# A gate of plain products, with the block sums of the next product made while it runs

## The chip, the cores and the metric

The kernel runs on one core of a Trainium2 chip. A core has five engines that work side by side and wait for one another by semaphores: TensorE (PE) multiplies matrices and puts the sums into PSUM, VectorE (DVE) and ScalarE (ACT) work on tiles of 128 partitions, GpSimd (POOL) does a few elementwise operations, and SyncE (SP) issues the transfers from memory. Each engine runs its own instructions strictly in the order of the program.

The metric is the device time of one execution in microseconds (us). The kernel before took 1316.55 us, the median of three runs from 1316.47 to 1319.54.

## The reference

Two decoder layers over 512 tokens of width D = 1024. Layer 0 mixes by a linear recurrence and a sparse attention, layer 1 by latent attention; both are followed by the same three steps, which are what matters here:

```python
for i in range(2):
    m = mixer_i(x)
    h = layer_norm(ALPHA * x + m, ln1_g[i], ln1_b[i])
    f = square(relu(h @ mlp_w1[i])) @ mlp_w2[i]                   # 1024 -> 4096 -> 1024
    e = sigmoid(h @ ple_w_gate[i]) * (p[i] @ ple_w_proj[i])       # the gate, and the embedding
    x = layer_norm(ALPHA * h + f + e, ln2_g[i], ln2_b[i])
```

Everything is in fp32.

## The kernel before

Activations are held transposed: a tile has 128 features as partitions and 512 tokens as columns. The residual is eight tiles `y[0]` to `y[7]`, which stay in SBUF. Steps that are split by tokens take a left and a right half of 256 columns (`H`).

A product in fp32 is made of three faster ones: each operand is split into a high part (a copy rounded to the faster type) and a low part (the rest), and PE adds high x high, high x low and low x high. Splits of weights are made on the chip: ACT casts the high part, DVE subtracts for the low one (L89, L90, L751, L752). Weights arrive as 1 MB tiles `wraw`; the pool `wp` has two buffers each for the raw tile, its high part `whi` and its low part `wlo`.

Two helpers multiply by weights.

- `gemm_t` (L113) makes plain products: a weight tile is a group of 48 matmuls of 512 columns, three (L107, L108, L109) for each of 8 row blocks k and 2 output tiles. With `lead` its first two groups run side by side, k by k, so that a product can start on the first operands that are ready; with `halves` holding "lead" those two groups run first on the left 256 columns and then on the right. `wload` (L88) loads and splits a weight tile, and is given a slightly higher priority (`ahead=30`).
- `seven` (L730) cuts weights and activations into 2 x 2 blocks and makes seven block products in place of eight, each of 12 matmuls of 256 columns (L786): 84 matmuls a group. Its operands are sums and differences of blocks. For the weights DVE makes them in `front` (a third pair of buffers in the pool `third` belongs to it), for the activations `Norm.blocks` makes them once. ACT and DVE add the products together again afterwards (L797 and the lines behind it).

`Norm` (L201) is the layer norm. The first norm of a layer (`norm a`) works by halves of tokens: a sum over features by PE (L256), which is taken off each `y` on DVE; squares on ACT, added on DVE (L252); statistics by PE (L269, two matmuls a half), a root on ACT, and a spread over partitions by PE (L283). Then `blocks` (L329) applies it: for each row block DVE scales (L350), ACT and DVE make the high and low part with the bias (L344, L345), ACT keeps h itself in `n_h` (L355), and POOL writes ALPHA x h into `y` (L356). When the right half is done, four row blocks of block differences follow, four instructions each (L361 to L364) and their splits (L341, L342). The seven operands lie in the tiles `xb`.

After the norm a layer runs: `embed` (p times `ple_w_proj`, kept in eight tiles `pp`, L821), then `mlp` (L841): the gate by `seven` in four groups with `evg` (tanh on ACT, a product with `pp` and a sum into `y` on DVE), then four parts, each `mlp_w1` by `seven` in four groups (`ev1`: relu and square on ACT, a split) and `mlp_w2` by `gemm_t` (`ev2`: a sum into `y`). In the last part `ev2` feeds `norm b`, which uses one pass over the sums and makes the h of the next layer.

Tiles of the seven-product operands take the places `h` had: pool `res` has 16 of them, pool `mp` 12. The end loop (L1089) opens the pools of a layer: `norm a`'s around the output projection and the embedding, then `norm b`'s and `third` around `mlp`.

The order of the work is the program's order on each engine, set by a scheduler at build time: what comes first in the code comes first, unless it isn't ready, and weights' splits are drawn forward by their priority (`high_priority(120)` in `seven`, 30 in `wload`). PSUM has six banks in rotation for products and two for the norm.

## Time and profile before

| | |
|---|---|
| median of three runs | 1316.55 us |
| profiled execution | 1319.66 us |
| its span | 1317.8 us |
| TensorE (PE) matmuls busy | 1228.2 us, 93% |
| PE weight loads (PEld, beside the matmuls) | 1083.4 us, 82% |
| VectorE (DVE) busy | 989.8 us, 75% |
| ScalarE (ACT) busy | 702.3 us, 53% |
| GpSimd (POOL) busy | 205.1 us, 16% |
| instructions | 19322 |

The span runs from the first instruction to the last; the 1.9 us by which the execution is longer lie around it. A busy share is an average over stages, and matmuls overlap: the next begins before the end of the one before is shown, so what a matmul costs is read from the distance of two starts. The granted clock (PEclk) is 1.00 at 2.4 GHz and 0.50 at 1.2 GHz. Instructions are named by the line of the kernel that makes them, and many lines are helpers.

### The profile page before, as it was taken

What the parts mean: (1) busy time and instruction counts of PE and PEld (TensorE: products, weight loads), DVE (VectorE), ACT (ScalarE), POOL (GpSimd) and SP (SyncE); (2) the same over time, 40 slices, a digit from 0 to 9 for tenths busy, and PEclk for the clock granted to TensorE, in tenths of its full rate; (3) what the DMA queues carried; (4) which work ended last, traced back from release to release, by engine and by line L of the source; (5) the groups of instructions that cost most, each with busy time, mean ns of one, the idle gap of its engine ahead of it and who ended that gap; (6) DMA issues with size and microseconds to landing.
All of it is one profiled execution on the core that took longest, in us unless ns stands there. A gap on an engine that the chain in (4) does not pass through costs nothing.

```text
span 1317.8 us, 19322 instructions
## 1 busy us (share of the span) xinstructions
PE 1228.2 (93%) x7400; PEld 1083.4 (82%) x7400; DVE 989.8 (75%) x1925; ACT 702.3 (53%) x1306; POOL 205.1 (16%) x237
## 2 busy tenths in 40 slices
PE   7997889399999999999899999994999999999998
PEld 6685678299889899898796888793998898998987
DVE  5799978999658376585838898679996584764857
ACT  4465765644526245263356988637455263452633
POOL 1457550100000000000544442101000000000000
PEclk9798999699999999999889999997999999999999
DMA  6221120033323223233112010120333232232311
GB/s 209 96 70 59 65 81 33 0 103 123 115 78 129 96 85 108 96 120 104 34 68 96 33 33 17 65 79 18 101 116 117 84 129 96 83 110 67 126 65 64
DMA packets 20925, 111.01 MB, mean 84 GB/s; under 512 B 2464, under 2 KB 6560, under 8 KB 8640
## 3 DMA queue, kind: packets, MB, share of 16 engines
q1 hardware_dynamic: 20736, 109.18, 24.6%
q8 instruction: 58, 0.95, 0.3%
q0 software_dynamic: 96, 0.59, 0.2%
q14 instruction: 35, 0.29, 0.1%
HBM read 107.66 MB, written 2.10 MB: 83 GB/s over the span
## 4 chain that ended last, share of the span: by engine, by line
PE 74%; DVE 16%; ACT 7%; issue 2%; DMA 0%; POOL 0%; ACTq 0%; SPq 0%; DVEq 0%; POOLq 0%
PE ps L786 29%; PE ps L107 12%; PE ps L108 12%; PE ps L109 12%; ACT l L408 2%; DVE mb L568 1%; DVE m L567 1%; PE ps L421 1%; DVE xb L342 1%; PE ps L897 1%; ACT whi L89 1%; PE ps L898 1%; PE ps L896 1%; DVE n_s L252 1%; DVE wlo L752 1%
## 5 line engine op out<-in xcount | busy, mean ns | idle before, releaser
L786 PE MATMUL ps<-xb,whi 128*128 128x256 f32 x1512 | 279.1, 286 | 0.2 <-ACT whi L751 0.2
L786 PEld LDWEIGHTS ps<-xb,whi 128*128 128x128 f32 x1512 | 239.4, 194 | 1.6 <-ACT whi L751 0.4
L786 PE MATMUL ps<-xb,wlo 128*128 128x256 f32 x756 | 215.0, 286 | 1.2 <-DVE wlo L752 1.2
L107 PE MATMUL ps<-ah,whi 128*128 128x512 f32 (+1 forms) x544 | 206.7, 380 | 0.0
L108 PE MATMUL ps<-al,whi 128*128 128x512 f32 (+1 forms) x544 | 206.5, 380 | 0.0
L109 PE MATMUL ps<-ah,wlo 128*128 128x512 f32 (+1 forms) x544 | 205.4, 378 | 0.0
L89 ACT CAST whi<-wraw 128x1024 fp32r<-128x1024 f32 (+3 forms) x146 | 122.1, 873 | 138.0 <-PE ps L108 114.4
L90 POOL TENSOR_TENSOR wlo<-wraw,whi 128x512 fp32r<-128x512 f32 (+2 forms) x54 | 93.4, 1747 | 456.4 <-ACT whi L89 456.4
L786 PE MATMUL ps<-xb,wh 128*128 128x256 f32 x728 | 131.7, 282 | 34.3 <-ACT u L797 17.5
L786 PEld LDWEIGHTS ps<-xb,wlo 128*128 128x128 f32 x756 | 146.4, 194 | 2.2 <-DVE wlo L752 2.2
L786 PEld LDWEIGHTS ps<-xb,wh 128*128 128x128 f32 x728 | 111.9, 190 | 35.4 <-ACT u L797 17.7
L869 DVE TENSOR_TENSOR y<-y,ps 128x512 f32<-128x512 f32 (+1 forms) x68 | 44.3, 654 | 128.3 <-PE ps L109 128.1
L751 ACT CAST whi<-wraw 128x512 fp32r<-128x512 f32 (+1 forms) x54 | 45.0, 832 | 158.3 <-PE ps L108 92.1
L107 PE MATMUL ps<-hh,whi 128*128 128x512 f32 (+1 forms) x304 | 112.7, 373 | 8.9 <-ACT hh L89 5.8
L108 PEld LDWEIGHTS ps<-al,whi 128*128 128x128 f32 x544 | 103.0, 189 | 19.9 <-DVE al L90 1.2
L107 PEld LDWEIGHTS ps<-ah,whi 128*128 128x128 f32 x544 | 102.9, 189 | 19.8 <-ACT ah L89 1.2
L109 PEld LDWEIGHTS ps<-ah,wlo 128*128 128x128 f32 x544 | 102.9, 189 | 18.7 <-issue 0.5
L109 PE MATMUL ps<-hh,wlo 128*128 128x512 f32 (+1 forms) x304 | 111.4, 369 | 6.7 <-POOL wlo L90 6.0
L108 PE MATMUL ps<-hl,whi 128*128 128x512 f32 (+1 forms) x304 | 112.8, 371 | 1.8 <-POOL hl L90 1.8
L90 DVE TENSOR_TENSOR wlo<-wraw,whi 128x1024 fp32r<-128x1024 f32 (+1 forms) x92 | 96.6, 1081 | 15.7 <-ACT whi L89 15.6
L786 PE MATMUL ps<-xb,wl 128*128 128x256 f32 x364 | 102.0, 281 | 1.0 <-DVE wl L752 1.0
L107 PEld LDWEIGHTS ps<-hh,whi 128*128 128x128 f32 x304 | 59.4, 196 | 19.4 <-ACT hh L89 6.4
(328 smaller groups left out, 2546.4 us busy)
## 6 DMA issues: line engine op xcount, KB each, us to landing
wraw<-in_mlp_w SPq DMA_DIRECT2D x64, 1024.0 KB, 4.8
wraw<-in_w_out SPq DMA_DIRECT2D x8, 1024.0 KB, 4.8
wraw<-in_w_gate SPq DMA_DIRECT2D x8, 1024.0 KB, 4.9
wraw<-in_w_in SPq DMA_DIRECT2D x6, 1024.0 KB, 4.8
wraw<-in_w_ukv SPq DMA_DIRECT2D x4, 1024.0 KB, 4.7
wraw<-in_w_in SPq DMA_DIRECT2D x16, 128.0 KB, 3.8
y<-in_xT SPq DMA_DIRECT2D x8, 256.0 KB, 4.0
wraw<-in_w_proj SPq DMA_DIRECT2D x2, 1024.0 KB, 4.8
```

Of the source, the lines that this page charges most:

```text
L89: (act or nc.scalar.copy)(hi, src)
L90: (sub or nc.vector.tensor_sub)(lo, src, f(hi))
L107: nc.tensor.matmul(ps, whi, xhi, start=start, stop=False)
L108: nc.tensor.matmul(ps, whi, xlo, start=False, stop=False)
L109: nc.tensor.matmul(ps, wlo, xhi, start=False, stop=stop)
L252: nc.vector.tensor_add(self.s2[:, cs], self.s2[:, cs], sq[:, cs])
L342: nc.vector.tensor_sub(t[:, H:], src, f(t[:, :H]))
L408: nc.scalar.activation(L[blk], L[blk], AF.Exp, bias=mx[:, NB + blk:NB + blk + 1], scale=self.scale, accum_out=sums[:, blk:blk + 1])
L421: nc.tensor.transpose(ps[t][:, c:c + P], self.L[blk][:, kb * P:(kb + 1) * P], ident)
L751: nc.scalar.copy(hi, src)
L786: nc.tensor.matmul(o, u[:, c], v, start=start and k == n == 0, stop=k == 3 and n == 2, skip_group_check=True)
L869: nc.vector.tensor_add(y[n][:, cs], y[n][:, cs], ps[:, cs])
```

## The change

- **The gate by plain products.** `mlp` calls `gemm_t` for the gate, with `lead=8, halves=("lead",)`: the first two of its four groups run side by side, first on the left 256 columns, then on the right, and the other two on all 512. Its operands are the high and low parts of h, which `norm a` now makes for all eight row blocks, in `res`, like `norm b`. The evaluation `evg` takes tanh and multiplies with `pp` by halves for the first four outputs.
- **Block differences during the gate.** `blocks` and `new_x` go. The new `Norm.sums` makes the four differences and their splits, of `y` as it is (scaled, without bias; where the bias doesn't cancel it is joined in the same instruction, `db` being the difference of two biases). `evg` calls it at output 3, right half. The other three operands of the seven products are halves of h's own tiles, so `product` takes pairs (`xh`, `xl`).
- **ALPHA joined to later sums.** POOL's multiplication goes for `norm a`. `y` becomes `ALPHA * y + pp` in one instruction of `evg`, and ALPHA times the bias (`ab`, made in `first`) is added with the sum of part 0's `mlp_w2`.
- **Pools.** `third` is opened in `mlp` and closed ahead of the last `mlp_w2`, where `norm b`'s pool then takes its memory.

```diff
@@ Norm.first @@
             if self.onepass:
                 self.centre()
+            else:
+                b = small[:, self.base + 8:self.base + 16]
+                self.db, self.ab = (const.tile([P, n], F32, name=nm("b")) for n in (4, 8))
+                nc.vector.tensor_sub(self.db, b[:, 4:], b[:, :4])
+                nc.vector.tensor_scalar_mul(self.ab, b, ALPHA)
@@ Norm.apply @@
-            if not self.onepass:
-                self.blocks(cs, rstd)
-                return
...
                 nc.scalar.activation(hi, yk, AF.Identity, bias=b)
                 nc.vector.scalar_tensor_tensor(lo, yk, b, f(hi), op0=OP.add, op1=OP.subtract)
-                nc.gpsimd.tensor_scalar(yk, yk, b, ALPHA, op0=OP.add, op1=OP.mult)
+                if self.onepass:
+                    nc.gpsimd.tensor_scalar(yk, yk, b, ALPHA, op0=OP.add, op1=OP.mult)
-        def blocks(self, cs, rstd):
...
+        def sums(self, xpool):
+            blocks = [[(hi[:, c], lo[:, c]) for hi, lo in self.h[r:r + 4]] for r, c in
+                      ((0, HALVES[0]), (4, HALVES[0]), (4, HALVES[1]))]
+            t = [[xpool.tile([P, S], F32R, tag=f"xt{i}{k}", bufs=1, name=nm("xt")) for k in range(4)] for i in range(4)]
+            b = small[:, self.base + 8:self.base + 16]
+            for k in range(4):
+                (b11, b12), (b21, b22) = ([y[i][:, c] for c in HALVES] for i in (k, k + 4))
+                v = [xpool.tile([P, S], F32, tag=f"al{4 + k % 2 * 2 + i}", bufs=1, name=nm("v")) for i in range(2)]
+                v = [u[:, c] for u in v for c in HALVES]
+                bk = b[:, k + 4:k + 5]
+                nc.vector.tensor_sub(v[0], b12, b11)
+                nc.vector.scalar_tensor_tensor(v[1], b22, bk, v[0], op0=OP.add, op1=OP.subtract)
+                nc.vector.scalar_tensor_tensor(v[2], b22, self.db[:, k:k + 1], b12, op0=OP.add, op1=OP.subtract)
+                nc.vector.scalar_tensor_tensor(v[3], b21, bk, v[1], op0=OP.add, op1=OP.subtract)
+                for i in (1, 2, 0, 3):
+                    split(t[i][k][:, :H], t[i][k][:, H:], v[i])
+            return blocks + [[(u[:, :H], u[:, H:]) for u in r] for r in t]
@@ mlp @@
-    def mlp(layer, xb, pp, mp, third, norm):
...
-        seven(a["w_gate"], [layer * 4 + g for g in range(4)], xb, mp, evg, third=third)
+    def mlp(layer, norm1, pp, mp):
+        h, xb, pools = norm1.h, [], ExitStack()
+        third = pools.enter_context(pool(f"third{layer}"))
+        def evg(n, ps, cs):
+            sg = mp.tile([P, S], F32, tag=f"ah{n % 2}", bufs=1, name=nm("sg"))[:, cs]
+            nc.scalar.activation(sg, ps[:, cs], AF.Tanh, scale=0.5)
+            nc.vector.scalar_tensor_tensor(pp[n][:, cs], sg, 1.0, pp[n][:, cs], op0=OP.add, op1=OP.mult)
+            if n == 3 and cs.start:
+                xb.extend(norm1.sums(mp))
+            for i in range(4) if n == 3 and cs.start else (n,) if n > 3 else ():
+                nc.vector.scalar_tensor_tensor(y[i], y[i], ALPHA, pp[i], op0=OP.mult, op1=OP.add)
+        gemm_t(a["w_gate"], [[layer * 4 + g] for g in range(4)], h, evg, lead=8, halves=("lead",))
@@ ev2 @@
-                nc.vector.tensor_add(y[n][:, cs], y[n][:, cs], ps[:, cs])
+                yn = y[n][:, cs]
+                if part == 0:
+                    nc.vector.scalar_tensor_tensor(yn, ps[:, cs], norm1.ab[:, n:n + 1], yn, op0=OP.add, op1=OP.add)
+                else:
+                    nc.vector.tensor_add(yn, yn, ps[:, cs])
...
+            if part == 3:
+                pools.close()
+                norm = Norm(pools.enter_context(pool(f"norm{layer}b", 1)), layer, 1, final=layer == 1)
             b = (layer * 2 + part // 2) * 8 + part % 2
```

How the queues change around the gate of layer 0 is shown at three places. On PE before, at the end of the embedding (`ph`, `pl`) and the start of the gate:

```order
L109 MATMUL ps_2354<-ph_2279,wlo_2284 128x512
L786 MATMUL ps_2385<-xb_2005,whi_2372 128x256 x2
L256 MATMUL ps_2112<-n_s_326_1880,cst 128x256
L786 MATMUL ps_2385<-xb_2005,wlo_2373 128x256
...
L786 MATMUL ps_2385<-xb_2023,wlo_2373 128x256
L269 MATMUL ps_2144<-cst,n_s_327_1881 128x1 x2
L283 MATMUL ps_2152<-cst,n_d_2148 128x128 x2
L786 MATMUL ps_2510<-xb_2005,wh_2497 128x256
L786 MATMUL ps_2385<-xb_2029,whi_2445 128x256 x2
```

The same engine and place now (`hh` and `hl` are the parts of h, L261, L274 and L288 the right half's mean, statistics and spread):

```order
L109 MATMUL ps_2250<-ph_2175,wlo_2180 128x512
L107 MATMUL ps_2279<-hh_2001,whi_2263 128x256
L108 MATMUL ps_2279<-hl_2002,whi_2263 128x256
...
L107 MATMUL ps_2287<-hh_2001,whi_2271 128x256
L261 MATMUL ps_2100<-n_s_328_1884,cst 128x256
...
L109 MATMUL ps_2291<-hh_2021,wlo_2272 128x256
L274 MATMUL ps_2132<-cst,n_s_329_1885 128x1 x2
L107 MATMUL ps_2287<-hh_2026,whi_2271 128x256
...
L288 MATMUL ps_2140<-cst,n_d_2136 128x128 x2
L109 MATMUL ps_2283<-hh_2031,wlo_2264 128x256
```

Between mean and statistics PE had ten products of the gate (rows with x2 are two); now some 60 products of the left half stand there, and six between the statistics and the spread.

On DVE before, at the end of the norm (block differences of the last row block, L364, and their splits), where the weight sums of the gate's next group follow (`ws`, `wlo`):

```order
L364 TENSOR_TENSOR n_t_410_2254<-n_h_354_2003,n_t_408_2252 128x256
L342 TENSOR_TENSOR xb_2259<-n_t_408_2252,xb_2259 128x256
L342 TENSOR_TENSOR xb_2262<-n_t_409_2253,xb_2262 128x256
L342 TENSOR_TENSOR xb_2268<-n_t_410_2254,xb_2268 128x256
L765 TENSOR_TENSOR ws_2374<-wraw_2370 128x512
L768 TENSOR_TENSOR ws_2374<-wraw_2370 128x512
L766 TENSOR_TENSOR ws_2374<-ws_2374,wraw_2370 128x512
```

On DVE now, behind the differences that `sums` makes during the gate (L830 is `ALPHA * y + pp`, L826 the product with `pp`, L90 the low half of the gate's fourth weight tile, L729 and L742 to L746 the weight sums of part 0):

```order
L830 SCALAR_TENSOR_TENSOR y_69<-y_69,pp_2212 128x512
L746 TENSOR_TENSOR ws_2715<-wraw_2711,ws_2715 128x512
L830 SCALAR_TENSOR_TENSOR y_70<-y_70,pp_2221 128x512
L826 SCALAR_TENSOR_TENSOR pp_2230<-sg_2612,pp_2230 128x512
L90 TENSOR_TENSOR wlo_2646<-wraw_2647,whi_2645 128x1024
L729 TENSOR_TENSOR wlo_2714<-wraw_2711,whi_2713 128x512
L729 TENSOR_TENSOR wlo_2714<-ws_2715,whi_2713 128x512
L729 TENSOR_TENSOR wlo_2714<-ws_2715,whi_2713 128x1024
L830 SCALAR_TENSOR_TENSOR y_71<-y_71,pp_2230 128x512
L90 TENSOR_TENSOR wlo_2646<-wraw_2647,whi_2645 128x1024
```

The fourth weight tile's low half now stands behind the differences, the sums into `y` and the weight sums of part 0.

On ACT before, where the table of tanh is loaded (L845; the casts are weights of the second group):

```order
L751 CAST whi_2570<-wraw_2495 128x1024
L751 CAST whi_2570<-ws_2499 128x512
L845 ACT_TABLE_LOAD
L845 ACTIVATE c_2443<-ps_2385 128x256
L797 COPY u_459_2523<-ps_2510 128x256
```

On ACT now (L282 is the root of the right half's statistics, L327 its high parts, L825 tanh of the left half's first output):

```order
L282 ACTIVATE n_d_2136<-n_d_2136 128x2
L327 ACTIVATE hh_2001<-y_67,small 128x256
L327 ACTIVATE hh_2006<-y_68,small 128x256
L825 ACT_TABLE_LOAD
L825 ACTIVATE sg_2370<-ps_2279 128x256
L327 ACTIVATE hh_2011<-y_69,small 128x256
L327 ACTIVATE hh_2016<-y_70,small 128x256
```

The table load and the first tanh have moved into the middle of the right half's norm, ahead of its third high part.

## Rows read from the trace of the kernel before

**Rows 1.** The page: shares of the chain that ended last, by engine.

```profile
PE 74%; DVE 16%; ACT 7%; issue 2%; DMA 0%; POOL 0%; ACTq 0%; SPq 0%; DVEq 0%; POOLq 0%
```

**Rows 2.** Waits of PE at the two norms: total us, times, longest.

```profile
PE ps L786 <- ACT wh L751: 16.8, 1, 16.8
PE ps L269 <- DVE n_s L252: 5.0, 1, 5.0
...
PE ps L786 <- ACT u L797: 17.5, 1, 17.5
```

**Rows 3.** Timeline of PE, layer 0: start us, us, instruction, [idle before <-releaser].

```profile
233.39 0.40 PE L786 MATMUL ps<-xb,whi 128*128 128x256 f32 x2
...
260.87 0.58 PE L786 MATMUL ps<-xb,wh 128*128 128x256 f32 x1 [16.80 <-ACT wh L751]
```

**Rows 4.** Timeline of DVE, both layers; L848 from the chain.

```profile
238.96 1.21 DVE L752 TENSOR_TENSOR wlo<-wraw,whi 128x1024 fp32r<-128x1024 f32 x1
240.09 0.41 DVE L252 TENSOR_TENSOR n_s<-n_s,n_sq 128x256 f32<-128x256 f32 x1
...
252.04 0.41 DVE L361 TENSOR_TENSOR n_t<-n_h 128x256 f32<-128x256 f32 x1
...
254.72 0.41 DVE L361 TENSOR_TENSOR n_t<-n_h 128x256 f32<-128x256 f32 x1
...
290.92 1.21 DVE c L848 x2
...
888.22 0.47 DVE L350 SCALAR_TENSOR_TENSOR y<-y,small,ps 128x256 f32<-128x256 f32 x1
888.61 0.52 DVE L345 SCALAR_TENSOR_TENSOR xb<-y,small,xb 128x256 fp32r<-128x256 f32 x1
889.06 0.47 DVE L350 SCALAR_TENSOR_TENSOR y<-y,small,ps 128x256 f32<-128x256 f32 x1
```

**Rows 5.** Windows: length; busy (count) of PE, PEld, DVE, ACT, POOL; clock, DMA, GB/s.

```profile
261.00:267.00 6.00, 6.00 (x28) 5.95 (x29) 5.07 (x9) 2.27 (x4) 0.00 (x0) 0.51 0.46 149
```

**Rows 6.** Windows: in the gate, and in part 1's `mlp_w2`.

```profile
277.00:287.00 10.00, 10.00 (x84) 9.90 (x84) 10.00 (x18) 3.58 (x6) 0.00 (x0) 1.00 0.32 107
430.00:472.00 42.00, 42.00 (x187) 34.79 (x186) 16.53 (x21) 9.02 (x12) 0.00 (x0) 1.00 0.19 69
```

**Rows 7.** Windows: gate and part 0's seven products, in each layer.

```profile
233.40:344.86 111.46, 87.48 (x684) 85.29 (x683) 103.85 (x198) 64.07 (x117) 4.48 (x10) 0.88 0.25 84
899.38:1004.07 104.69, 84.96 (x682) 83.40 (x680) 97.92 (x184) 60.26 (x107) 3.34 (x8) 0.90 0.24 81
```

**Rows 8.** Timeline of PE, both widths of matmuls; 388.69 from the chain.

```profile
210.06 0.28 PE L108 MATMUL ps<-hl,whi 128*128 128x256 f32 x1
...
217.26 0.28 PE L108 MATMUL ps<-hl,whi 128*128 128x256 f32 x1
...
388.69 40.05 PE ps L786 x336
...
852.13 0.39 PE L107 MATMUL ps<-hh,whi 128*128 128x512 f32 x1
...
860.29 0.39 PE L107 MATMUL ps<-hh,whi 128*128 128x512 f32 x1
```

**Rows 9.** Timeline of PE: statistics of the left half.

```profile
224.71 0.50 PE L269 MATMUL ps<-cst,n_s 128*128 128x1 f32 x4
...
226.10 0.60 PE L283 MATMUL ps<-cst,n_d 128*128 128x128 f32 x4
```

**Rows 10.** Timeline of ACT: a weight cast, and the load of tanh's table.

```profile
233.68 1.03 ACT L751 CAST whi<-wraw 128x1024 fp32r<-128x1024 f32 x1
...
271.16 1.28 ACT L845 ACT_TABLE_LOAD   x1
272.46 0.38 ACT L845 ACTIVATE c<-ps 128x256 f32<-128x256 f32 x1
```

**Rows 11.** DMA issues: count, KB each, us from issue to landing.

```profile
wraw<-in_w_gate SPq DMA_DIRECT2D x8, 1024.0 KB, 4.9
```

More of the change, by code (lines that the diff above doesn't have):

```diff
@@ L201, in hybrid_kernel, with __init__ @@
     class Norm:
-        def __init__(self, pool, layer, which, final=False, xpool=None):
-            self.pool, self.final, self.onepass, self.xpool = pool, final, which == 1, xpool
+        def __init__(self, pool, layer, which, final=False):
+            self.pool, self.final, self.onepass = pool, final, which == 1
             self.base = C_LN + layer * 32 + which * 16
@@ L368, in new_x @@
-        def new_x(self, j, k):
-            n = 4 * j + k
-            if n < 12:
-                return self.xpool.tile([P, S], F32R, tag=f"xb{n}", bufs=1, name=nm("xb"))
-            n -= 12
-            return res.tile([P, S], F32R, tag=f"h{'hl'[n % 2]}{n // 2}", name=nm("xb"))
+                if self.onepass:
[17 more added lines that the diff above has]
+            return blocks + [[(u[:, :H], u[:, H:]) for u in r] for r in t]
@@ L839, in embed @@
         return pp
-    def mlp(layer, xb, pp, mp, third, norm):
-        def evg(g, c11, t):
-            nc.scalar.activation(t[:, H:], t[:, H:], AF.Tanh, scale=0.5)
-            nc.scalar.activation(t[:, :H], c11, AF.Tanh, scale=0.5)
-            for i in range(2):
-                n, r = 2 * g + i, t[:, i * S:(i + 1) * S]
-                nc.vector.scalar_tensor_tensor(r, r, 1.0, pp[n], op0=OP.add, op1=OP.mult)
-                nc.vector.tensor_add(y[n], y[n], r)
-        seven(a["w_gate"], [layer * 4 + g for g in range(4)], xb, mp, evg, third=third)
+    def mlp(layer, norm1, pp, mp):
[10 more added lines that the diff above has]
+        gemm_t(a["w_gate"], [[layer * 4 + g] for g in range(4)], h, evg, lead=8, halves=("lead",))
         for part in range(4):
@@ L1097, in hybrid_kernel @@
             with pool(f"norm{layer}a", 1) as npool:
-                norm = Norm(npool, layer, 0, xpool=mp)
+                norm = Norm(npool, layer, 0)
                 if layer == 0:
@@ L1103, in hybrid_kernel @@
                 pp = embed(layer, mp)
-            with pool(f"norm{layer}b", 1) as npool, pool(f"third{layer}") as third:
-                xb, norm = norm.xb, Norm(npool, layer, 1, final=layer == 1)
-                mlp(layer, xb, pp, mp, third, norm)
-                h = norm.h
+            h = mlp(layer, norm, pp, mp)
 def _chunks(w, ncols, kk, kgroup=None):
```

38 lines of the change are left out of this document (4 added, 34 removed).

## The prediction, made before the changed kernel ran

> **What bounds the kernel now.** I read the chain that ended last first: three quarters of it is TensorE (PE) [rows 1], so what counts is where PE stands still or works for too long. The waits of PE name two great holes, one in each layer, 16.8 and 17.5 us, both just after the norm that precedes the gate; the first comes with 5.0 us of wait for the norm's own statistics [rows 2]. The timeline of layer 0 shows the whole hole: the gate's first product starts at 233.39, twelve products (a first batch of 12, over in 2.5 us) use only the left half of the columns, and then nothing but eight tiny statistics matmuls stands before the next product at 260.87 [rows 3]. In those 25 us VectorE (DVE) normalises the right half and makes 16 block differences and their 16 splits, 2.68 us for each of four row blocks at 0.335 us an instruction [rows 4]. Behind the hole the granted clock is 0.51 for some 6 us in which 28 products run at 0.214 us each instead of 0.12 [rows 5]. Then the gate runs as seven block products, PE and DVE both full (10.00 of 10 us) [rows 6].
>
> I measure the change on one stretch in each layer, from the first product of the gate to the first matmul of the first `mlp_w2`: gate plus the four seven-product groups of part 0. It took 111.46 us in layer 0 and 104.69 us in layer 1 [rows 7]. Outside it the order of every engine is the same but for single neighbours.
>
> **The change part by part.** I rebuild the stretch from its work and its new waits.
>
> PE's work. The gate's first two groups come in halves: 2 x 96 matmuls of 256 columns. Sixty of that width stand between 210.06 and 217.26, 0.120 us each, so 192 take 23.0 us. The other two groups are 96 matmuls of 512 columns; 36 of those stand between 852.13 and 860.29, 0.2267 us each, so 21.8 us. Part 0 keeps its 336 products, 40.05 us as in part 1 [rows 8]. Before, the gate too was 336 products, so plain products cost 23.0 + 21.8 - 40.05 = 4.7 us a layer more. Statistics of the second half now stand between products; at full clock they take about 0.36 us for each of three places [rows 9], 1.1 us. Work: 23.0 + 21.8 + 40.05 + 1.1 = 86.0 us a layer. All of it can start at the end of the embedding products, because the left half of h is ready then (the first twelve products of before already ran there).
>
> New waits of PE, layer 0, in order of the queue.
> - Second weight group: its buffer is held by the embedding products until 233.4; its cast started at 233.68 in before for the same reason and takes 1.03 us [rows 10]. Ten products of the first group (1.2 us) cover it but for 0.15.
> - Low halves of rows 4 to 7: DVE makes a low half (1.13 us [rows 4]), one h part, 13 instructions of centring and squares (13 x 0.335 = 4.4) and another 1.13, from 234.7 on: ready at 241.7. PE arrives after 56 products and one mean, at 240.6: 1.1 us.
> - Statistics: from the first to the second statistics matmul it took 1.39 us [rows 9]; six products and its own 0.36 stand between: 0.3.
> - Tanh stands on ScalarE (ACT) ahead of the right half's third h, and waits for the left half's first sum on PE. ACT then loads its table, 1.28 us, with the next ACTIVATE 1.30 behind the load's start [rows 10]. The third h is needed three products of k later and comes in time; the eighth sum's PSUM bank, which the second tanh frees, is 0.25 late. The Trainium skill, page "ScalarE: Activation LUTs", section "What ACT_TABLE_LOAD costs", gives about 1283 ns for the load and about 1380 ns of drain, some 2.66 us for a switch. The trace shows the load alone and no drain behind it; by the page the third h would come 1.4 us later, and an estimate of the sum by it would be up to 1.4 us less gain in layer 0.
> - Third group: both weight buffers are in use until the lead's last products, so its cast (1.03, behind two tanh) and its low half (1.13) come after: 1.35 + 0.4 = 1.75. In layer 1 four tanh halves stand between: 2.1.
> - Fourth group: DVE's queue. After the last h of the right half (252.8: statistics over at 245.0, which is 241.7 and ten products 1.2, 1.39, 0.3 and 0.36; then eight pairs of 0.84 for h, 6.7, and a low half, 1.13) stand ahead of its first low half: 8 gate halves at 0.39 (3.1), 16 differences (4 at 0.335, 12 at 0.39: 6.0), 16 splits (5.4), two low halves (2.3), five full-width sums at 0.605 (3.0), four weight sums of part 0 (2.4): 22.2 us [rows 4]. So it is ready at 275 + 1.1 = 276. PE is there at 259.1 (233.4, 24.1 of lead and statistics, 1.55 of the first three waits) + 1.75 + 10.9 + 1.9 (four full and eight hoisted products) = 273.7: wait 2.1. In layer 1 twice as many products of part 0 are hoisted and DVE is earlier: 0.4.
> - Part 0 itself: waits as before, about 1.1 and 0.6; its weights come by DMA 4.9 us after their buffer is free [rows 11], which is the split before, and that is early enough.
>
> Sums: layer 0 waits 0.15 + 1.1 + 0.3 + 0.25 + 1.75 + 2.1 + 1.1 = 6.8, stretch 92.8, gain 18.7. Layer 1, where the embedding ends later against the norm, 0.4 + 2.1 + 0.4 + 0.6 = 3.5, stretch 89.5, gain 15.2. Together **33.9 us**.
>
> Where the old stall goes: what is late next is the weights' low half on DVE, in the third and fourth group. DVE loses the seven-product work of the gate (4 groups x about 10.6 us by its instruction counts at the same prices) and gets 4.7 us a group instead, so it is no longer full through the gate, but only some 10% below PE.
>
> Edits with one answer: POOL's 16 multiplications a layer are gone; PE waits for none of them. Two tiny bias vectors a layer on DVE stand under the output projection. The bias times ALPHA joined to part 0's sums makes 8 sums two-operation ones, 0.605 us each [rows 4] and 4.8 in all at the most, in an `mlp_w2` in which DVE is busy for 16.53 of 42.00 us (part 1's is shown) [rows 6]. `norm b`'s pool now takes the memory of `third`: its first tile waits for the last readers there, which the operands of `mlp_w2` wait for anyway: 0, or 1 us if a weight tile's release is late. These and the waits above are the unknown: at the least zero wait in all (10.3 us more gain), at the most what the second case says.
>
> Against the profiled execution (1319.66 us, span 1317.8) the sum gives 1285.8. The median shown is 3.1 us lower, 1316.55; the stretch is no part of that difference, so 1316.55 - 33.9 = 1282.7, taken as **1283**.
>
> **The rivals.** *DVE becomes the bound.* The differences, splits and gate halves get no time while PE does the right half, since ACT's tanh, casts and DVE's sums hand values back and forth; then the 22.2 us start when the lead ends (259.1) and not at 252.8. PE waits 6.3 us a layer more: 33.9 - 12.6 = 21.3, time 1295. For it: DVE was full in the old gate, and its queue keeps order. Against: the same 32 instructions ran without a gap in before (0.335 each).
>
> *The change does not do what it says.* PE keeps order too, and the mean and statistics of the right half stand in the middle of the left half's products. If these come late, the left half's 96 products (11.5 us a layer) cover nothing: 33.9 - 23.0 = 10.9, time 1305.6. For it: DVE now has three low halves of weights among the squares. Against: the order has 53 to 66 products ahead of the statistics.
>
> *Slower than before.* PE's clock stays at the lower level (1.2 GHz) through the gate because it stands and starts again at each new wait. The gate is worth 768 products of 256 columns in both layers (a full-width one counts as two); at 0.214 instead of 0.12 each loses 0.094, 72 us in all, time 1355. It decides from 33.9 / 0.094 = 360 products, nearly half the gate, at the lower level. Against: after a hole of 25 us only 28 ran so, and no new wait is over 2.1 us.
>
> **How the numbers follow.** Forecast 0.75, DVE as bound 0.14, no cover 0.05, low clock 0.02; 0.02 for a gain above 44 us, 0.02 for one lost elsewhere to within 0.3% (some 4 us, about what a measurement of this kernel can tell from no change). The range holds the forecast with no waits at all (1272.4, unlikely in full, so 1274) up to DVE as bound and a little (1297). Faster by over 0.3%: 0.95; within: 0.03; slower: 0.02.
>
> **What would show it.** Right: no wait of PE over 3 us between the embedding and the first `mlp_w2`; the granted clock 1.00 there; the stretch 90 to 95 us in both layers; PE's longest waits on weights' low and high halves (the helper's lines), near 2 us each. DVE as bound: waits of 5 us or more on the fourth group's low half, or DVE at 10.0 of 10 through the gate. No cover: a wait of 5 us for the statistics. Wrong altogether if the stretches shrink and the time does not, which would mean that another stretch has grown.

## The result, and the profile after

The changed kernel takes 1284.87 us (median of four runs, 1283.70 to 1286.41) against 1316.62 for the kernel before, run beside it: a ratio of 0.9754, 95% interval 0.9736 to 0.9772. The forecast was 1283 in a range from 1274 to 1297.

The profiled execution took 1283.7 us, with a span of 1281.9. The engines' busy time stands beside the table of before, and the shares of the chain that ended last answer to [rows 1]:

```profile
PE 1232.4 (96%) x7304; PEld 1081.1 (84%) x7304; DVE 947.6 (74%) x1849; ACT 679.9 (53%) x1258; POOL 191.0 (15%) x205
PE 75%; DVE 15%; ACT 7%; issue 2%; DMA 0%; POOL 0%; POOLq 0%; ACTq 0%; SPq 0%; DVEq 0%
```

PE works 4 us more than before and is busy for 96% in place of 93%: the time went out of PE's holes, not out of its work. The two stretches from the first gate product to the first matmul of the first `mlp_w2`, in the windows view (length; busy time and count of PE, PEld, DVE, ACT, POOL; clock, DMA share, GB/s), answer to [rows 7]:

```profile
233.19:325.39 92.20, 89.24 (x636) 83.20 (x634) 82.54 (x160) 52.53 (x97) 0.00 (x0) 1.00 0.28 92
879.40:967.53 88.13, 86.72 (x634) 82.27 (x632) 77.86 (x146) 50.20 (x90) 0.00 (x0) 1.00 0.31 108
```

From 111.46 and 104.69 us they fell to 92.20 and 88.13, by 19.26 and 16.56, together 35.8 us; the two spans differ by 35.9. Everything outside moved by 0.1 us in all. The granted clock is 1.00 throughout, where before it was 0.88 and 0.90. PE's waits in the two stretches, layer 0 first (releaser: total us, times, longest), answer to [rows 2]:

```profile
PE ps L109 <- DVE wlo L90: 1.4, 2, 0.9
PE ps L107 <- ACT whi L89: 1.0, 1, 1.0
PE ps L763 <- ACT whi L728: 0.4, 1, 0.4
...
PE ps L109 <- DVE wlo L90: 1.0, 1, 1.0
PE ps L107 <- ACT whi L89: 0.4, 1, 0.4
```

In place of 16.8 and 17.5 us there are waits of 1 us at the most, and all of them are for a split of weights. The timeline of PE shows where they stand, three in layer 0 and two in layer 1 (start us, us, instruction, [idle before <-releaser]):

```profile
241.63 0.50 PE L109 MATMUL ps<-hh,wlo 128*128 128x256 f32 x2 [0.92 <-DVE wlo L90]
...
259.14 0.28 PE L109 MATMUL ps<-hh,wlo 128*128 128x256 f32 x1
260.38 0.50 PE L107 MATMUL ps<-hh,whi 128*128 128x512 f32 x1 [0.97 <-ACT whi L89]
...
275.48 0.50 PE L109 MATMUL ps<-hh,wlo 128*128 128x512 f32 x1 [0.49 <-DVE wlo L90]
...
903.99 0.50 PE L107 MATMUL ps<-hh,whi 128*128 128x512 f32 x1 [0.39 <-ACT whi L89]
...
906.21 0.49 PE L109 MATMUL ps<-hh,wlo 128*128 128x512 f32 x1 [1.01 <-DVE wlo L90]
```

They are the low halves of rows 4 to 7 (241.63), the third weight tile (260.38, and 903.99 with 906.21) and the fourth (275.48). The idle time in brackets is shorter than the gap, because the matmul before it is shown to its modelled end: from 259.14 to 260.38 are 1.24 us, where 0.12 would do. Just ahead of the last wait of layer 0 stand eight products of part 0, and one of them waits for part 0's own weights (L763, 0.4 us).

### The profile page after: what moved, and what is told of

It reads as the page before. It is cut to its first block, busy times and chain, and to the rows that moved or that the text cites. A ratio compares the mean times of both kernels' runs of the same rounds, so it can differ in the third digit from the quotient of the medians.

```text
span 1281.9 us, 18923 instructions
## 1 busy us (share of the span) xinstructions
PE 1232.4 (96%) x7304; PEld 1081.1 (84%) x7304; DVE 947.6 (74%) x1849; ACT 679.9 (53%) x1258; POOL 191.0 (15%) x205
## 4 chain that ended last, share of the span: by engine, by line
PE 75%; DVE 15%; ACT 7%; issue 2%; DMA 0%; POOL 0%; POOLq 0%; ACTq 0%; SPq 0%; DVEq 0%
PE ps L763 25%; PE ps L109 14%; PE ps L107 14%; PE ps L108 14%; ACT l L385 2%; DVE mb L545 2%; DVE m L544 1%; PE ps L398 1%; DVE hl L328 1%; PE ps L887 1%; ACT whi L89 1%; PE ps L888 1%; DVE wlo L90 1%; PE ps L886 1%; DVE n_s L257 1%
## 5 line engine op out<-in xcount | busy, mean ns | idle before, releaser
L107 PE MATMUL ps<-hh,whi 128*128 128x512 f32 (+1 forms) x496 | 173.1, 352 | 10.6 <-ACT hh L89 6.2
L109 PE MATMUL ps<-hh,wlo 128*128 128x512 f32 (+1 forms) x496 | 171.4, 350 | 9.1 <-POOL wlo L90 5.7
L108 PE MATMUL ps<-hl,whi 128*128 128x512 f32 (+1 forms) x496 | 173.3, 351 | 1.1 <-POOL hl L90 1.1
L90 POOL TENSOR_TENSOR wlo<-wraw,whi 128x512 fp32r<-128x512 f32 (+2 forms) x54 | 93.4, 1746 | 490.6 <-ACT whi L89 490.6
L90 DVE TENSOR_TENSOR wlo<-wraw,whi 128x1024 fp32r<-128x1024 f32 (+1 forms) x108 | 116.1, 1102 | 15.1 <-ACT whi L89 14.8
L763 PE MATMUL ps<-xt,whi 128*128 128x256 f32 x680 | 125.2, 284 | 0.4 <-ACT whi L728 0.4
L107 PEld LDWEIGHTS ps<-hh,whi 128*128 128x128 f32 x496 | 95.6, 194 | 24.1 <-ACT hh L89 6.8
L109 PEld LDWEIGHTS ps<-hh,wlo 128*128 128x128 f32 x496 | 95.6, 194 | 22.3 <-POOL wlo L90 6.9
L108 PEld LDWEIGHTS ps<-hl,whi 128*128 128x128 f32 x496 | 95.9, 194 | 14.1 <-POOL hl L90 2.5
L763 PEld LDWEIGHTS ps<-xt,whi 128*128 128x128 f32 x680 | 106.0, 192 | 1.4 <-ACT whi L728 0.7
L763 PE MATMUL ps<-xt,wlo 128*128 128x256 f32 x340 | 95.9, 283 | 0.0
L763 PE MATMUL ps<-hl,whi 128*128 128x256 f32 x260 | 73.5, 283 | 0.0
L763 PE MATMUL ps<-hh,whi 128*128 128x256 f32 x260 | 73.5, 283 | 0.0
```

The source lines that it names most:

```text
L90: (sub or nc.vector.tensor_sub)(lo, src, f(hi))
L107: nc.tensor.matmul(ps, whi, xhi, start=start, stop=False)
L108: nc.tensor.matmul(ps, whi, xlo, start=False, stop=False)
L109: nc.tensor.matmul(ps, wlo, xhi, start=False, stop=stop)
L763: nc.tensor.matmul(o, u[:, c], v, start=start and k == n == 0, stop=k == 3 and n == 2, skip_group_check=True)
```

## The experiments

The first table gives for every kernel its median, and the two stretches of its profiled execution (from the end of the embedding to the first `mlp_w2`), read from the timeline of PE.

| kernel | median us | layer 0 | layer 1 |
|---|---|---|---|
| before | 1316.6 | 111.5 | 104.7 |
| changed | 1284.87 | 92.2 | 88.1 |
| changed again | 1284.51 | 93.2 | 88.1 |
| full-width lead | 1303.46 | 101.2 | 97.4 |
| differences twice | 1306.97 | 104.5 | 99.3 |
| third tile in the third buffer | 1285.08 | 93.7 | 87.0 |
| higher priority for tiles 3 and 4 | 1280.79 | 89.5 | 87.3 |
| both | 1277.61 | 88.7 | 86.2 |
| low halves by POOL | 1296.20 | 98.2 | 94.8 |
| no join, POOL scales | 1293.24 | 96.2 | 93.4 |
| idle work on POOL | 1290.56 | 95.6 | 89.9 |
| no join, ACT scales | 1287.54 | 95.5 | 87.7 |
| priority, no join (POOL) | 1285.21 | 91.5 | 91.1 |
| priority, idle work on POOL | 1282.77 | 91.7 | 88.9 |

The baseline of the comparisons is the changed kernel's second row, 1284.51 us, whose interval against before was 0.9744 to 0.9773.

### The changed kernel once more

No edit.

> The changed kernel once more, unaltered, as the base for the runs beside it. Theory (what separates the two traces, 35.9 us, from the two medians, 31.75 us, is a scatter of one execution of either kernel): the median lies between 1283.7 and 1286.4 us, and in its trace the two stretches from the first gate product to the first mlp_w2 matmul are 92.2 and 88.1 us to within 0.3, while the scatter stands elsewhere. Rival (the scatter lies in the new stretches, since their waits vary from execution to execution): the stretches differ by 1 us or more from 92.2 and 88.1.

Measured: 1284.51 us (1284.48 to 1286.93), span of the profiled execution 1285.1, that is 3.2 us above the first. Layer 0's stretch took 93.2 us, 1.0 more, with two new gaps of 0.4 and 0.7 us in part 0; layer 1's was the same; between the two stretches it took 555.8 us in place of 554.0. So both hold in part: the larger part of the scatter lies outside, but layer 0's new stretch scatters by 1 us too, more than the 0.3 that the theory allowed.

### How much the left half's products cover

```diff
-        gemm_t(a["w_gate"], [[layer * 4 + g] for g in range(4)], h, evg, lead=8, halves=("lead",))
+        gemm_t(a["w_gate"], [[layer * 4 + g] for g in range(4)], h, evg, lead=8)
```

In `evg` the condition on the right half goes as well.

> The gate's first two groups run on all 512 columns and not first on the left half: nothing of the gate can then run before the right half's first h. Theory (the left half's products as a cover are worth most of the gain, the differences that left the path the rest): PE stands from the end of the embedding to the right half's first h, about 14 us in layer 0 and 8 to 9 in layer 1, runs behind that at the lower granted clock for some products (2.6 us, as behind the old hole), and saves 1.2 us by wider products and up to 1.9 and 0.3 us of waits: 11 to 12 us more in layer 0 and 8 to 10 in layer 1, so 1303 to 1308 us. Rival (what counts is that the block differences left the path, 11 us a layer, and the cover adds little): 1285 to 1295 us.

Measured: 1303.46 us, 19 us above the changed kernel, as the theory had it. The timeline of PE gives the first gate product of either layer, and the windows view the stretch behind the hole of layer 1:

```profile
248.02 1.65 PE L107 MATMUL ps<-hh,whi 128*128 128x512 f32 x3 [1.11 <-ACT hh L327]
...
900.66 1.65 PE L107 MATMUL ps<-hh,whi 128*128 128x512 f32 x3 [1.12 <-ACT hh L327]
...
900.60:907.00 6.40, 6.34 (x16) 5.02 (x17) 6.40 (x17) 3.58 (x10) 0.00 (x0) 0.54 0.00 0
```

The embedding ended at 233.7 and 891.1, so the holes are 14.3 and 9.6 us, and behind the second 16 products of full width took 0.40 us each at a clock of 0.54, in place of 0.2267. The cover is thus worth 19 of the 32 us, the slower products behind the holes included. The 13.6 us that are left against before (1317.11 in these runs) are put down to the differences that left the path, less the dearer plain products; that is what remains by subtraction, and no run shows these two one by one.

### Whether DVE has room

```diff
-            for k in range(4):
+            for k in (0, 1, 2, 3, 0, 1, 2, 3):
                 (b11, b12), (b21, b22) = ...
```

> The 16 block differences and 16 splits of a layer are made twice over into the same tiles, on DVE and ACT, at the place where they stand: on DVE 11.4 us more in each layer (6.0 + 5.4 us). Theory (DVE's queue sets when the low half of the gate's fourth weight tile is ready, in layer 0 1.9 us too late and in layer 1 0.2 us before PE comes, so that DVE has no room left there): 9 to 11.4 us more in each layer, 1303 to 1308 us, as one wait of PE for that low half. Rival (over the whole stretch DVE is busy for 82.5 of 92.2 us and 77.9 of 88.1, so about 10 us a layer are free to take the work): 1 to 2 us more in each layer, 1287 to 1289 us.

Measured: 1306.97 us, 22.5 above the changed kernel; the stretches are 12.3 and 11.2 us longer. PE's waits behind the lead, layer 0 and layer 1:

```profile
PE ps L109 <- DVE wlo L90: 8.0, 1, 8.0
PE ps L107 <- ACT whi L89: 3.1, 2, 2.2
...
PE ps L109 <- DVE wlo L90: 5.2, 1, 5.2
PE ps L107 <- ACT whi L89: 3.1, 2, 2.2
```

The third tile's low half starts on DVE at 273.07 us, in the changed kernel (second row) at 260.44:

```profile
273.07 1.22 DVE L90 TENSOR_TENSOR wlo<-wraw,whi 128x1024 fp32r<-128x1024 f32 x1
...
260.44 1.22 DVE L90 TENSOR_TENSOR wlo<-wraw,whi 128x1024 fp32r<-128x1024 f32 x1
```

The size is the theory's, and the 10 us that the busy share (82.5 of 92.2 us) seemed to leave free were mostly not to be had. The way is another. The long waits (8.0 and 5.2 us) are for the third tile's low half, behind the doubled differences, and not for the fourth's, for which PE waits some 0.2 us in layer 0 and not at all in layer 1; and 3.1 us a layer are for the third tile's cast on ACT, which has the casts of the doubled differences ahead of it. All gaps of PE together grew by 10.1 us in layer 0 and 7.6 in layer 1. The rest of the 12.3 and 11.2 us are products that ran slower behind the waits, since the granted clock had fallen to its lower level there (see "What the join is worth"). That the sum comes so near to 11.4 us in both layers is in part chance.

### A place in the queue, or a buffer

Three runs. The first draws the splits of the gate's third and fourth weight tile forward:

```diff
-                part(g, c, wload(dram, idx, sub=sub, ahead=ahead), byn)
+                part(g, c, wload(dram, idx, sub=sub, ahead=later or ahead), byn)
...
-        gemm_t(..., lead=8, halves=("lead",))
+        gemm_t(..., lead=8, halves=("lead",), later=120)
```

> The splits of the gate's third and fourth weight tiles get the higher priority that those of the seven products have, so that on DVE the fourth tile's low half stands before the last differences and not behind the sums into y and the weight sums of part 0. Theory (that low half is late by its place in DVE's queue alone): layer 0's wait of 1.9 us for the fourth group goes, the waits for the third group (1.6 and 1.95 us) stay, 1.5 to 2 us less than the changed kernel beside it. Rival (DVE's sum of work sets the end, whatever the order): the wait comes back at part 0's first products, within 0.5 us of the changed kernel.

Measured: 1280.79 us, 3.7 less, more than either case. Layer 0's wait for the fourth tile went, as the theory said; besides, the third tile's cast and low half, drawn forward on ACT and DVE too, came earlier, and its gaps fell from 1.6 to 1.0 us in layer 0 and from 1.9 to 1.1 in layer 1. That their buffer alone had set them was wrong.

The second gives the third tile the buffers that stand empty, without the priority:

```diff
             for cs in HALVES if "lead" in halves else (ALL,):
+                if third and cs.start:
+                    w3 = wload(dram, idxs[2][0], sub=sub, ahead=ahead, third=third)
...
-        hi = wp.tile([P, 2048], F32R, tag="whi", name=nm("whi"))
-        lo = wp.tile([P, 2048], F32R, tag="wlo", name=nm("wlo"))
+        if third:
+            hi, lo = (third.tile([P, 2048], F32R, tag=f"w3{u}", bufs=1, name=nm("w" + u)) for u in "hl")
```

> The third weight tile's parts take the empty third pair of buffers; no higher priority. Theory (DVE's queue sets the end in layer 0, a buffer in layer 1): layer 0's wait of 1.6 us for the third group goes and that for the fourth grows by about as much, while layer 1 gains its 1.95 us; together 1.5 to 2.5 us less than the changed kernel (1284.5). Rival (the waits are each a cost of its own and add up): 3.6 us less, with layer 0's stretch at about 90.6 us.

Measured: 1285.08 us, no gain (1283.03 to 1287.06). In layer 0 the wait for the third tile is gone and that for the fourth has taken all of it:

```profile
PE ps L109 <- DVE wlo L90: 1.4, 2, 0.9
...
PE ps L112 <- DVE wlo L90: 3.7, 2, 2.7
```

(The changed kernel above, two waits of 0.9 and 0.5; this one below, with 0.9 and 2.7, where L112 is the same line of the helper. The 0.9 of rows 4 to 7 is the same in both.) The low half of the fourth tile stands at the same place of DVE's queue, and PE only comes there earlier. Layer 1 gained 1.1 us, not 1.95; a product of part 0 waited 0.5 us in its place. The waits do not add up. Joined into one they cost more, for behind the wait of 2.7 us seven products of full width came every 0.43 us, 1.4 us more than at the full clock.

The third run has both edits.

> As the run with the higher priority; besides, the third weight tile's high and low part take the third pair of weight buffers, which stand empty during the gate, so that its split needn't wait for the end of the lead. Theory (the third group waits for a buffer, the fourth for DVE's queue): the waits of 1.6 and 1.95 us for the third group go too, 4.5 to 5.5 us less than the changed kernel beside it, 1279 to 1281 us, and no wait of PE above 0.5 us behind the right half's norm in either layer. Rival (DVE's sum of work sets the end): at most 2 us less, with new waits in part 0.

Measured: 1277.61 us (1276.20 to 1279.06), 6.9 less than the changed kernel, and against before a ratio of 0.9702 (0.9687 to 0.9716): the fastest of all. Its stretches in the windows view, and the only wait of PE in them:

```profile
233.86:322.53 88.67, 87.67 (x636) 82.99 (x634) 82.19 (x160) 53.19 (x97) 0.00 (x0) 1.00 0.28 96
873.81:959.97 86.16, 86.16 (x634) 82.33 (x633) 77.63 (x146) 50.30 (x90) 0.00 (x0) 1.00 0.32 111
...
PE ps L112 <- DVE wlo L90: 0.9, 1, 0.9
```

DVE is busy for as long as in the changed kernel (82.19 against 82.54 us), and PE no longer stands still in layer 1. So it was not the sum of DVE's work that set these 6.9 us, but its order and a buffer: with the buffer alone the fourth tile's low half stays behind the differences, with the priority alone the third tile's split still waits for the lead to give its buffers free. The stretches account for 5.5 to 6.5 of the 6.9 us; the rest is within the scatter.

### Taking work from DVE to POOL

```diff
-                    split(t[i][k][:, :H], t[i][k][:, H:], v[i])
+                    split(t[i][k][:, :H], t[i][k][:, H:], v[i], sub=nc.gpsimd.tensor_sub)
```

> The low halves of the 16 splits of the block differences are subtracted by POOL and not by DVE: DVE has 5.4 us less in each layer, POOL 16 instructions of 256 columns more, 0.65 to 0.9 us each by half of its 1.28 to 1.75 us for 512 columns. Theory (DVE's work ahead of the fourth tile's low half sets layer 0's wait of 1.9 us): that wait goes, 1.5 to 2 us less than the changed kernel (1284.5), nothing in layer 1. Rival (POOL is too slow for it, its last split comes at 268 us or later, and the first products of part 0 wait): 1 to 5 us more in each layer.

Measured: 1296.20 us, 11.7 more. The theory falls, and the rival has the sign but not the way: the products of part 0 did not wait, those of the gate did, 4.4 us for the third tile's cast in layer 0. The timelines of DVE and POOL in layer 0, and below two such rows of DVE in the changed kernel:

```profile
254.94 0.96 DVE L346 SCALAR_TENSOR_TENSOR v<-y,small,v 128x256 f32<-128x256 f32 x1
255.82 0.95 DVE L347 SCALAR_TENSOR_TENSOR v<-y,b,y 128x256 f32<-128x256 f32 x1
256.70 0.95 DVE L348 SCALAR_TENSOR_TENSOR v<-y,small,v 128x256 f32<-128x256 f32 x1
...
253.53 10.80 POOL L90 TENSOR_TENSOR xt<-v,xt 128x256 fp32r<-128x256 f32 x12 [57.89 <-ACT xt L89]
...
256.42 0.48 DVE L347 SCALAR_TENSOR_TENSOR v<-y,b,y 128x256 f32<-128x256 f32 x1
256.81 0.48 DVE L346 SCALAR_TENSOR_TENSOR v<-y,small,v 128x256 f32<-128x256 f32 x1
```

While POOL subtracts, 0.90 us an instruction, DVE's starts are 0.88 us apart in place of 0.39: the two take turns. DVE's instructions themselves last 0.95 us with no idle time between them, so they don't stand for a buffer. DVE thus lost about as much as the 5.4 us of subtractions that it was spared; ACT's casts of the differences came every 0.88 us too, and the third tile's cast stands behind them. Of the 11.7 us, 5.4 are products at the lower clock behind these waits.

### What the join is worth

The join is undone: POOL makes (y + bias) x ALPHA behind the differences.

```diff
+            if n == 3 and cs.start:
+                for i in range(KT):
+                    b = small[:, norm1.base + 8 + i:norm1.base + 9 + i]
+                    nc.gpsimd.tensor_scalar(y[i], y[i], b, ALPHA, op0=OP.add, op1=OP.mult)
             for i in range(4) if n == 3 and cs.start else (n,) if n > 3 else ():
-                nc.vector.scalar_tensor_tensor(y[i], y[i], ALPHA, pp[i], op0=OP.mult, op1=OP.add)
+                nc.vector.tensor_add(y[i], y[i], pp[i])
```

In `ev2` part 0's sum is a plain one again.

> The scale and bias of the residual are not joined to later sums: POOL makes (y + bias) x ALPHA for all eight tiles behind the block differences (8 instructions of 512 columns, about 1.2 us each by its 0.6 us for 256), the sums into y are plain sums. Theory (the join is worth nothing, POOL's work is covered): within 1 us of the changed kernel (1284.5). Rival (the sums into y stand on DVE ahead of the fourth tile's low half, and wait for POOL): 1 to 3 us more in each layer, 1286.5 to 1290.5 us.

Measured: 1293.24 us, 8.7 more, worse than either case. PE's waits behind the lead in layer 0, and rows of DVE and POOL:

```profile
PE ps L107 <- ACT whi L89: 4.1, 2, 2.6
...
256.62 0.83 DVE L347 SCALAR_TENSOR_TENSOR v<-y,b,y 128x256 f32<-128x256 f32 x1
257.37 0.91 DVE L346 SCALAR_TENSOR_TENSOR v<-y,small,v 128x256 f32<-128x256 f32 x1
...
254.40 4.70 POOL L832 TENSOR_SCALAR y<-y,small 128x512 f32<-128x512 f32 x3 [57.88 <-ACT xt L89]
259.53 0.98 POOL L832 TENSOR_SCALAR y<-y,small 128x512 f32<-128x512 f32 x1 [0.44 <-DVE v L348]
```

It is not the sums into `y` that waited: PE's waits are for the third tile's split. Two causes were possible. POOL slows DVE again (0.75 to 0.83 us from start to start, and POOL itself takes 1.57 an instruction in place of 0.98). And eight more instructions in the program had moved the third tile's low half six places back in DVE's queue, since its priority reaches only so far ahead. Four more runs bear on this.

Idle work on POOL, with the join as in the changed kernel:

```diff
+            for k in range(8):
+                z = xpool.tile([P, S], F32, tag="zz", bufs=1, name=nm("zz"))
+                nc.gpsimd.tensor_scalar(z, f(t[0][k % 4]), 1.0, ALPHA, op0=OP.add, op1=OP.mult)
             return blocks + ...
```

> The changed kernel, and POOL besides makes eight multiplications of 512 columns into a tile that nobody reads, from the block differences as they come: as much work of POOL as without the join, at about the same place, with nobody waiting for it. Theory (POOL's work slows DVE beside it, 0.75 to 0.83 us for a two-input sum of 256 columns that takes 0.39 alone, and the low half of the third and fourth tile come late): 6 to 9 us more than the changed kernel (1284.5), so 1290 to 1294, with the same waits of 2.5 to 3 us for the third group's split. Rival (without the join DVE waited for POOL's results): within 1 us of the changed kernel.

Measured: 1290.56 us, 6.0 more, though nobody waits for POOL's result. The low half had moved back by the same six places here.

No join, but ACT scales:

```diff
-                    nc.gpsimd.tensor_scalar(y[i], y[i], b, ALPHA, op0=OP.add, op1=OP.mult)
+                    nc.scalar.activation(y[i], y[i], AF.Identity, bias=norm1.ab[:, i:i + 1], scale=ALPHA)
```

> The join undone in another way: ACT, not POOL, makes ALPHA x y + ALPHA x bias, eight instructions of 512 columns, some 0.6 us each. Theory (the join by itself is worth nothing; what cost 8.7 us was POOL at work beside DVE): within 2 us of the changed kernel (1284.5), since ACT is busy for 52.5 of 92.2 us. Rival (the sums into y wait on DVE for whoever scales y): 5 us or more above it.

Measured: 1287.54 us, 3.0 more: between the two cases. POOL does nothing here, and the low half stands seven places further back; layer 0 is 2.3 to 3.3 us longer and layer 1 is not. That was the place in the queue, which the theory had left out, but not by the wait alone. PE waits 2.4 us for the third tile's low half, and in return not for the fourth tile, which had 1.9 us of gaps. What is left over is the clock behind that wait (timeline of PE and windows view; the last two lines are the run with the priority and no join, layer 1):

```profile
264.05 0.79 PE L109 MATMUL ps<-hh,wlo 128*128 128x512 f32 x1 [2.36 <-DVE wlo L90]
264.64 0.63 PE L107 MATMUL ps<-hh,whi 128*128 128x512 f32 x1
265.07 0.63 PE L108 MATMUL ps<-hl,whi 128*128 128x512 f32 x1
...
264.00:270.00 6.00, 5.95 (x15) 4.71 (x16) 6.00 (x14) 5.34 (x10) 0.00 (x0) 0.54 0.50 175
...
906.22 0.80 PE L109 MATMUL ps<-hh,wlo 128*128 128x512 f32 x1 [1.51 <-DVE wlo L90]
906.20:910.00 3.80, 3.78 (x10) 3.02 (x11) 3.80 (x5) 1.92 (x5) 1.58 (x1) 0.56 0.43 114
```

The products come every 0.43 us in place of 0.2267, at the clock's lower level. Each loses 0.2 us, and 12 of them make 2.4 of the 3.0 us. No expectation of these runs but that of the full-width lead had this cost. Counted in the same way it is 5.8 us of the doubled differences' 22.5 (29 products), 5.4 of the 11.7 with the low halves by POOL (27), 4.9 of the 8.7 without the join (25), 1.4 of the idle work's 6.0 (7), and none in the changed kernel, with the priority or with both edits. The longest wait alone does not decide it: behind waits of 0.6 and 1.8 us in layer 1 of the idle work the clock stayed at 1.00, behind the 1.3 and 1.5 us ahead of the last line above it fell.

Then both of POOL's versions with the edit of the priority run on top, which puts the low halves back to the front. First without the join:

> The join undone by POOL, now with the higher priority for the gate's third and fourth tile. In the run without it, the eight more instructions in the program had also moved the third tile's low half six places back in DVE's queue; with the priority it stands where the run with the priority alone (1280.8) has it. Theory (of the 8.7 us the place in the queue made about 3, which ACT's version cost too, and POOL at work beside DVE the rest, which stays): 1284 to 1287 us. Rival (it was all the place of the low half): within 1.5 us of 1280.8.

Measured: 1285.21 us, 4.4 above the priority alone. And the idle work on POOL with that priority:

> The same with the eight multiplications by POOL that nobody reads, and the join as in the changed kernel. Theory (POOL beside DVE slows it, whoever reads the result): 1282.5 to 1285 us against 1280.8 with the priority alone, some 3 us less of loss than without the priority. Rival (all of the 6 us was the place of the low half): within 1.5 us of 1280.8.

Measured: 1282.77 us, 2.0 above the priority alone, at the lower end of the theory. The median is a poor measure here, since the four runs lie in two pairs 2 us apart (1281.66 and 1281.80, 1283.74 and 1283.78). By the two stretches of the profiled executions it is 3.7 us (91.7 and 88.9 against 89.5 and 87.3), and without the join 5.8 (91.5 and 91.1). So of the 8.7 us that undoing the join cost, 4.4 by the medians (5.8 by the stretches) came with POOL at work, and the rest went with the place of the low halves in DVE's queue, most of it as products at the lower clock. POOL's work that nobody reads makes 3.7 of the 5.8 us. Of the 2.1 that remain, 1.4 are the seven products at the lower clock in layer 1 that are shown above, which the idle work's run does not have; DVE waits for a result of POOL nowhere in these two stretches.

## Why the prediction was right, step by step

The stretches can be taken apart as the forecast built them. A gap is the distance of two starts on PE beyond 0.12 us (256 columns), 0.2267 (512) or 0.09 (statistics); work is what is left.

| term | layer 0, forecast | measured | layer 1, forecast | measured |
|---|---|---|---|---|
| work | 86.0 | 86.3 | 86.0 | 85.8 |
| second weight group | 0.15 | 0.42 | - | - |
| low halves of rows 4 to 7 | 1.1 | 1.18 | - | - |
| statistics | 0.3 | 0.34 | 0.4 | 0.28 |
| tanh and its bank | 0.25 | 0 | - | - |
| third group | 1.75 | 1.64 | 2.1 | 1.94 |
| fourth group | 2.1 | 1.89 | 0.4 | 0 |
| part 0 | 1.1 | 0.42 | 0.6 | 0.12 |
| stretch | 92.8 | 92.2 | 89.5 | 88.1 |

**Work.** The durations of [rows 8] hold for the new products: 86.3 and 85.8 us.

**The old stall, and what is late next.** It is the weights' low half on DVE, as the forecast said, and for the third tile its high half on ACT, which the forecast had in the same sum. DVE's queue was followed row by row there, and came out so: the last low part of h ends at 252.6 (forecast 252.8), the fourth tile's low half starts at 274.2 (forecast 274.9, 276 less its 1.1):

```profile
252.15 0.48 DVE L328 SCALAR_TENSOR_TENSOR hl<-y,small,hh 128x256 fp32r<-128x256 f32 x1
...
274.19 1.23 DVE L90 TENSOR_TENSOR wlo<-wraw,whi 128x1024 fp32r<-128x1024 f32 x1
```

Of the fourth group's 1.89 us, 1.1 stand ahead of the low half, at products of part 0 that wait for their own weights. The forecast had those products in the queue but not their wait; as PE stood there, it waited the less for the low half, and the sum came out the same. The run with doubled differences confirms that this queue sets the time: 11.4 us of added work on DVE made PE's gaps 10.1 and 7.6 us longer, at the third tile's split, and the slower products behind them made up the rest.

**The cover.** The forecast put 23 us on the left half's products if nothing waits; without them 19 us were lost.

**Tanh.** ACT loads its table ahead of the right half's third high part, and the third part came in time: no gap of PE above 0.12 us there.

```profile
246.99 1.28 ACT L825 ACT_TABLE_LOAD   x1
248.28 0.39 ACT L825 ACTIVATE sg<-ps 128x256 f32<-128x256 f32 x1
```

The next ACTIVATE starts 1.29 us behind the load's start. The Trainium skill, page "ScalarE: Activation LUTs", section "What ACT_TABLE_LOAD costs", counts about 2.66 us with a drain; here the load alone is seen, as in [rows 10], and the measurement decides.

**What was mis-sized.** Part 0's waits (1.1 and 0.6 us) were carried over from before and came out at 0.4 and 0.1, though in the second execution layer 0 had 1.5 us of them. "Edits with one answer: POOL's multiplications, PE waits for none of them" was right for the kernel before and asked the wrong question: what counts is whom POOL slows. Had the multiplications gone with the differences into the gate, they would have cost 8.7 us. That they were joined to later sums is what keeps POOL still there, so the join is no side matter of this change.

**The median.** The sum was made on the stretches and taken off the median shown: 1316.55 - 33.9. The stretches gave 35.8, 2 us more, yet the medians are only 31.75 us apart. The profiled execution of before was the longest of its own (1319.54 of 1316.47 to 1319.54), that of after the shortest; in the second profile of the changed kernel the stretches gave 34.8. So the forecast's 33.9 is 1 to 2 us too small by the stretches and 2 us too large by the medians, and how near 1283 came to 1284.87 owes something to this scatter. The kernels here scatter by 1 to 4 us, and the last section shows where a part of it lies.

**The signs.** Three of the four came: no wait over 3 us, the clock at 1.00, and the longest gaps, 1.6 to 1.9 us, at splits of weights. The fourth did not in layer 1: its stretch is 88.1 us, under the 90 to 95 that were named, and the forecast's own 89.5 was under them too.

**The rivals.** DVE as bound: no wait of 5 us came, and the runs with priority and buffers show that DVE's order and a buffer, and not its sum, set the 6.9 us that were left. No cover: the statistics are 0.3 us late, not 5. Low clock: 1.00 in both stretches, but its mechanism is real: in the runs with longer waits 7 to 29 products ran at the lower level.

## What to carry to other kernels

When an engine's long stretch of preparation stands between two products, look for products whose operands are ready earlier (here half of the columns), put them into the hole, and move the preparation beside the products that follow, even where these become dearer by some microseconds. Then read the feeding engine's queue row by row: a small piece that the busy engine waits for, such as a weight's low half, must stand ahead of the long work that nobody needs yet, and a buffer or a priority alone may only shift the wait. Moving elementwise work from VectorE to GpSimd may take nothing off VectorE if both then run at the same time; here it cost 11.7 us. And count more than the wait itself when a small piece comes late: where the granted clock falls behind it, the products that follow can cost as much again.

## What the runs showed of the hardware that was not expected

**DVE and POOL take turns.** Beside a two-input subtraction of POOL, DVE's two-input sums of 256 columns start every 0.88 us in place of 0.39, and POOL's subtractions take 0.90 us each; beside POOL's scaling by 512 columns some of them start 0.75 to 0.83 us apart, and POOL's own instruction takes 1.57 us in place of 0.98. The Trainium skill, page "SBUF — State Buffer", section "SBUF: two separate sides", says that the two engines share a pair of ports by an exclusive lock for the whole of an instruction, held by a DVE instruction with two inputs in SBUF against a POOL instruction that reads SBUF, and that the loser blocks. The times agree with that in kind: in 0.88 us each of the two starts one instruction. How long POOL's subtraction takes alone no run shows, so whether each is shut out for the whole of the other's isn't shown. The kernel before shows it in its norm, where L356 of POOL is short: L345 of DVE takes 0.61 us beside it, and 0.48 where POOL is idle.

```profile
246.86 0.48 DVE L345 SCALAR_TENSOR_TENSOR xb<-y,small,xb 128x256 fp32r<-128x256 f32 x1
...
248.42 0.61 DVE L345 SCALAR_TENSOR_TENSOR xb<-y,small,xb 128x256 fp32r<-128x256 f32 x1
...
248.32 0.44 POOL L356 TENSOR_SCALAR y<-n_h 128x256 f32<-128x256 f32 x1 [0.42 <-ACT xb L344]
```

**The granted clock falls in some profiles and not in others, for the same work.** Behind the thin stretch at the end of layer 0's `norm b` the changed kernel's profile has a clock of 0.56 for 7 us, and the run with the priority 1.00 over the same work, which has the same order there (windows, changed kernel first):

```profile
640.00:647.00 7.00, 7.00 (x25) 6.09 (x26) 3.33 (x12) 1.11 (x3) 0.24 (x1) 0.56 0.00 0
...
637.30:644.30 7.00, 7.00 (x39) 5.92 (x40) 5.06 (x16) 3.20 (x10) 1.11 (x2) 1.00 0.00 1
```

PE did 25 matmuls in the one and 39 in the other; the time between the two stretches is 554.0 us in the one and 551.3 in the other. Of the other eleven profiles of the changed kernel and its variants nine have the fall at this place and two have not. The three without it all have the priority's edit (one with that edit has the fall), so that the profiles alone don't tell the program from the execution. That one program can do both is likely from the two pairs of runs of the priority with idle work: the pair at 1281.7 us has a mean clock of 0.984 over the whole execution, the pair at 1283.8 one of 0.980. What makes it fall stays open; it is of the size of the scatter of the kernels here.
